# Low parts of the input weights kept in DRAM in the first half and loaded from there in the second

## Chip, cores and metric

The kernel runs on one core of a Trainium2 chip. The metric is the time of one execution on the device in microseconds (us). Three runs of the kernel before took 2506.31, 2506.98 and 2509.43 us.

## What is computed

One step of a streaming encoder layer with 1024 prompt tokens and 32 tokens of a running stream, model width 2048. Cut to what matters here:

```
xn   = rms_norm(x, norm_g)
proj = xn @ w_in                     # 2048 x 8320: q, k, v, gates, RWKV r/k/v, LoRA
q, k = rope(rms_norm(q)), rope(rms_norm(k))
att  = diff_attention(q, [past_k, k], [past_v, v])      # chunked causal mask
rw   = RWKV-7 recurrence over r, k, v, decay, a         # solved in chunks of 64 tokens
out  = x + [att * silu(g_att) ; rw * silu(g_rw)] @ w_out
```

All is float32 at the interface.

## The kernel before

**Tiling.** The tokens are cut into two halves: A has 544 tokens (512 of the prompt and the 32 of the running stream), B has 512. Columns of `w_in` come in 65 tiles of 128 (`f` = 0 to 64), those of `w_out` in 16. A projection of one tile (`proj`) multiplies the 16 x 128 rows of `w_in` into a PSUM bank `pj`. Half A is projected in two chunks of 288 and 256 tokens (`CHUNKS`), half B in one of 512. Both operands are split into a rounded high part of type fp32r and the rest, also fp32r; each of the 16 steps is three matmuls: high weight by high x (`wh`, `xh`), high weight by low x (`wh`, `xl`), low weight by high x (`wl`, `xh`).

**Weights.** The 16 steps come in four groups. For each group `load_w` (L238) loads 128 x 512 raw weights into `wr` (two slots) on the POOL queue, and `split_w` makes `wh` on ACT (L234) and `wl` on VectorE (L235), three slots each. So a group is 12 matmuls per chunk, and a slot of `wh` or `wl` comes free when TensorE is through with the group three before. Every tile of `w_in` is loaded and split twice, once in each half: 2 x 65 x 4 = 520 groups. Those of `w_out` for half A go the same way (64 groups); for half B `load_w2` loads pairs.

```
def split_w(raw):
    wh = T([128, 4, 128], "wh", F32R, bufs=3)
    wl = T([128, 4, 128], "wl", F32R, bufs=3)
    S.copy(wh, raw)
    V.tensor_tensor(wl, raw, wh.bitcast(F32), op=ALU.subtract)
```

**Order of the work.** Sixteen units (`u`), eight of each half, follow one another; unit `u` projects q, k, v, the attention gate, r, k, v and the RWKV gate of head pair `i`. Between the groups of a projection `pump` emits pieces of attention and of the recurrence of this and the unit before, by hand-set latencies (`LAT`) on a clock `clk` that counts TensorE's work. A scheduler then orders each engine's queue; `load_w` has high priority in it. An engine's queue is in order: an instruction that waits holds all behind it. SP issues nearly all transfers other than raw weights (`dma`, L184, and `dmq`, L112).

**The recurrence.** In `rw_down` each unit has two parts (`sub`). Products of TensorE are masked into `MM` (L784); 32 x 32 blocks of it go out to DRAM (`dm`), come back four times as `ms`, and VectorE inverts them in 31 steps of two instructions, `tm` (L803) and `ts` (L805), from a start `ts<-tinit`. The result goes out as `dt` (four stores) and comes back as `TT`, `t0q` and `t1q` for `rw_chain`, whose matmuls write the bank `ch`. `ms`, `ts` and `TT` have one slot each.

**Keys.** `qk_task` rotates q and k with a copy of rows (`t<-t`), and sends the low part of k into `Ks` by two copies (`Ks<-t`, L112); the score matmuls `sc<-Ks,Qd` read that.

**Between the halves.** At the end of unit 7 the normed x of half B is loaded (`t<-xB`) and split in place of A's, then the LoRA tile (`f` = 56) of half B is projected. Spans below are microseconds from the start of the execution: half A's projections run to about 1060, half B's to about 2085, then `w_out` follows for A and for B.

Of the kernel before, what the change touches and what calls it, by code (L numbers as in the profile page):

```python
# [12 lines left out]
F32R = mybir.dt.float32r  # L13
# [6 lines left out]
D = 2048  # L20
# [26 lines left out]
def build(tc, I, O):  # L47
    nc = tc.nc
# [7 lines left out]
    def T(shape, tag, dt=F32, bufs=1):  # L56
        cnt[0] += 1
        return sb.tile(shape, dt, tag=tag, name=f"{tag}_{cnt[0]}", bufs=bufs)
# [122 lines left out]
    def dma(out, in_):  # L181
        if out.dtype == F32R:
            out, in_ = out.bitcast(F32), in_.bitcast(F32)
        nc.sync.dma_start(out, in_)  # L184
# [35 lines left out]
    for z in (Qlo, wulo, TTb):  # L220
        G.memset(z.bitcast(F32), 0.0)

    mixd = [dr.tile([16, 128, n], F32, name=f"mixd{i}") for i, n in enumerate((NA, NB))]
    kpast = dr.tile([NH, 128, 2, 512], F32R, name="kpast")
    Spast = dr.tile([NP, 128, 64], F32, name="Spast")
# [5 lines left out]
# [4 lines that stand above are left out]
        V.tensor_tensor(wl, raw, wh.bitcast(F32), op=ALU.subtract)  # L235
        return wh, wl

    def load_w(wsrc, g, q=nc.gpsimd):  # L238
        with tc.high_priority():
            raw = T([128, 4, 128], "wr", bufs=2)  # L240
            q.dma_start(raw, wsrc[:, g * 512:(g + 1) * 512].rearrange("p (k f) -> p k f", k=4))  # L241
            return split_w(raw)

    def load_w2(wsrc, g):
        with tc.high_priority():
# [16 lines left out]

    RAW = ["Ks", "Vt", "E0", "E1", "rsg", "AR", "BK", "ms", "UV", "rk", "ca", "MM", "AR", "P3", "v", "rsg"]
    BUFS = dict(AR=2, MM=2, rsg=2, t=4)
    wpre = {0: load_w(I["w_in"][56], 0, nc.sync)}
    raw = []
    acc = T([128, NA], "asg")
    for k, tag in enumerate(RAW):
        xr = T([128, NA], tag, bufs=BUFS.get(tag, 1))
        dma(xr, I["xA"][:, k, :])  # L270
        raw.append(xr)
        if k % 4 == 0 and k < 8:
            wpre[k // 4 + 1] = load_w(I["w_in"][56], k // 4 + 1, nc.sync)
        split_x(k, xr, col(P_NG, k))
    for k, xr in enumerate(raw):
        s2 = T([128, NA], "p3", bufs=P3B) if k else acc
# [78 lines left out]
            p, r = (t.rearrange("p (a b) -> p a b", b=blocks) for t in (p, r))  # L355
        V.tensor_tensor(out, p, r, op=ALU.mult)

    def proj(wsrc, chunks, ws=None, nxt=None, pairs=False, banks=None):
        banks = banks or [PT("pj", 3) for _ in chunks]
        if len(chunks) == 2:  # L360
            order = [(0, 0), (0, 1), (1, 0), (1, 1), (0, 2), (0, 3), (1, 2), (1, 3)]
        else:
            order = [(0, g) for g in range(4)]
        ws = ws or {}
        for o, (b, g) in enumerate(order):
            if g not in ws:
                if pairs:
                    ws.update(load_w2(wsrc, g))
                else:
                    ws[g] = load_w(wsrc, g)  # L370
            wh, wl = ws[g]
            c0, n = chunks[b]
            for k in range(4 * g, 4 * g + 4):
                for m, (w, x) in enumerate(((wh, XH), (wh, XL), (wl, XH))):
                    mm(banks[b][:, :n], w[:, k % 4, :], x[k][:, c0:c0 + n],
                       start=(k == 0 and m == 0), stop=(k == KT - 1 and m == 2))
                if k < KT - 1:
                    if k % 4 == 3 or (k % 2 == 1 and n == 512):
                        pump()
                    else:  # L380
                        chs.run()
            if nxt and all(g != h for _, h in order[o + 1:]):
                for k in range(4 * g, 4 * g + 4):
                    nxt(k)
        return [(banks[b], c0, n) for b, (c0, n) in enumerate(chunks)]
# [17 lines left out]
    low, high = slice(0, 64), slice(64, 128)  # L403
# [263 lines left out]
    def lora(half, ws=None):  # L667
        ncnk = (9, 8)[half]
        spare = scores2()
        banks = proj(I["w_in"][56], CHUNKS[half], ws, banks=None if half else [spare[:, 0, :], spare[:, 1, :]])  # L670
        Lt = T([128, ncnk, 64], "p3", bufs=P3B)
        shift_tile(half, ncnk, banks, 24, Lt)
        S.activation(Lt[0:64], Lt[0:64], AF.Tanh)
        tc.keep_in_program_order(S.preload_act_table_set("natural_log_exp_and_others"))
        W = ncnk * 64
        Lf = Lt.rearrange("p c t -> p (c t)")
        Ls = T([128, 2, W], "lora", F32R)
        ll = T([128, W], "p3", F32R, bufs=P3B)
        for w in range(2):
            rows = (low, high)[w]  # L680
            S.copy(Ls[rows, w, :], Lf[rows])
            V.tensor_tensor(ll[rows], Lf[rows], Ls[rows, w, :].bitcast(F32), op=ALU.subtract)
        dma(Ls[64:128, 0, :], ll[0:64])
        dma(Ls[0:64, 1, :], ll[64:128])
        return Ls
# [311 lines left out]
    def out_proj(half, f, nxt=None):  # L997
        n = (NA, NB)[half]
        xr = T([128, n], "t", bufs=4)
        dma(xr, I["xA" if half == 0 else "xB"][:, f, :])  # L1000
        for (p, c0, m) in proj(I["w_out"][f], CHUNKS[half], nxt=nxt, pairs=half == 1):
            V.tensor_tensor(xr[:, c0:c0 + m], p[:, :m], xr[:, c0:c0 + m], op=ALU.add)
        dma(O["yA" if half == 0 else "yB"][f], xr)

# [15 lines left out]
    for u in range(16):  # L1020
        half, i = divmod(u, 8)
        n, ncnk, chunks = (NA, NB)[half], (9, 8)[half], CHUNKS[half]
        if u == 8:
            rb_b()
            ready["am"] = clk[0]
            load_rope(1)
            drain(los, ("decay", 7))
            Lt = lora(1)
        sa = dict(offs=[0, 128, 288, 416] if half == 0 else [0, 128, 256, 384])
        sr = dict()  # L1030
        srs.append(sr)
        los.add(("decay", u), rw_decay(half, i, sr, Lt))
        for sub in range(2):
            dns.add(("down", u, sub), rw_down(half, i, sub, sr))
            chs.add(("chain", u, sub), chain_when_down(half, i, sub, sr))
            pos.add(("post", u, sub), rw_post(half, i, sub, sr))

        def q_stage():
            banks = proj(I["w_in"][i], chunks)
            qks.add(("q", u), qk_task(0, half, i, qk_start(0, banks, n), sa))  # L1040

        def k_stage(prev):
            banks = proj(I["w_in"][8 + i], chunks)
            drain(qks, (prev, u))
            qks.add(("k", u), qk_task(1, half, i, qk_start(1, banks, n), sa))

        def v_stage(prev):
            banks = proj(I["w_in"][16 + i], chunks)
            drain(qks, (prev, u))
            qks.add(("v", u), v_task(half, i, banks, sa))  # L1050

        def ga_stage():
            banks = proj(I["w_in"][24 + i], chunks)
            if u:
                drain(ats, ("att", u - 1))
            sg = T([128, n], "asg")
            silu(sg, banks)
            sa["sg"] = sg

        def rw_stage(t):  # L1060
            banks = proj(I["w_in"][32 + 8 * t + i], chunks)
            if t == 0:
                if u:
                    drain(dns, ("down", u - 1, 1))
                sr["rk_"] = T([128, 2, ncnk, 64], "rk")
            rk = sr["rk_"]
            if t < 2:
                shift_tile(half, ncnk, banks, 8 * t + i, rk[:, t])
                if t == 1:
                    if half == 0:  # L1070
                        G.memset(rk[:, 1, 8, 32:64], 0.0)
                    sr["rk"] = rk
                return
            if u:
                drain(chs, ("vread", u - 1))
            v = T([128, ncnk, 64], "v")
            shift_tile(half, ncnk, banks, 16 + i, v)
            sr["v"] = v

        def gr_stage():  # L1080
            banks = proj(I["w_in"][57 + i], chunks,
                         nxt={7: source(I["xB"], True), 15: source(mixd[0], False)}.get(u))
            if u > 1:
                drain(pos, ("post", u - 2, 1))
            sg = T([128, n], "rsg", bufs=2)
            silu(sg, banks)
            sr["sg"] = sg

        att_stages = [(q_stage,), (v_stage, "q"), (k_stage, "v")] if half == 0 else [
            (q_stage,), (k_stage, "q"), (v_stage, "k")]  # L1090
        for stage, *args in att_stages:
            stage(*args)
            pump()
        ats.add(("att", u), att_task(half, i, sa))
        if u == 5:
            ats.add("stats", stats_task())
        ga_stage()
        drain(qks, ("k" if half == 0 else "v", u))
        pump()
        for t in range(3):  # L1100
            rw_stage(t)
            pump()
        gr_stage()
        pump()
# [109 lines left out]
```

## Time and profile before

| | us |
|---|---|
| runs, median of three (lowest to highest) | 2506.98 (2506.31 to 2509.43) |
| profiled execution | 2504.47 |
| its span | 2502.7 |
| TensorE (PE) busy | 2443.2 |
| VectorE (DVE) busy | 1864.0 |
| ACT busy | 1370.3 |
| moved by DMA | 286.72 MB |

Busy time is the time in which at least one instruction of the engine was under way. Matmuls are pipelined and their ends are modelled, so that TensorE can pause for a tenth of a microsecond or two without a gap in its busy time. A wait is put down to what came last before the waiting instruction started.

### The profile page before, as it was taken

How to read it: one execution, taken by the hardware profiler on the slowest of the kernel's cores; microseconds unless marked ns; L12 is line 12 of the kernel's file. 1: busy time of each engine (PE TensorE's matmuls, PEld its weight loads, DVE VectorE, ACT ScalarE, POOL GpSimd, SP SyncE). 2: the span in 40 equal slices, each digit the busy share in tenths (PEclk: the TensorE clock that was granted, in tenths of full speed). 3: DMA queues.
4: the chain of work that ended last, by engine and by line, in shares of the span. 5: the costliest groups of instructions: out<-in, count | busy, mean ns of one | idle time of the engine just before them, and what ended most of it. 6: DMA issues, size and time to landing. Idle time of an engine off the chain costs nothing.

```text
span 2502.7 us, 49026 instructions
## 1 busy us (share of the span) xinstructions
PE 2443.2 (98%) x17124; PEld 2163.9 (86%) x17124; DVE 1864.0 (74%) x5716; ACT 1370.3 (55%) x3286; POOL 453.8 (18%) x1070
## 2 busy tenths in 40 slices
PE   8999999999999999999999999999999999999999
PEld 7999999999999999977777787878787878999887
DVE  7577778788877878778888787878787878643432
ACT  7446465655556665656655565656565656332321
POOL 1212121211212121211111112121211111111100
PEclk9999999999999999999999999999999999999999
DMA  5343333434243525353333333333333344544443
GB/s 181 107 119 90 93 104 96 118 86 120 85 121 123 151 74 149 103 147 94 111 90 95 106 98 103 97 107 90 108 95 109 92 126 146 171 152 136 139 149 104
DMA packets 198919, 286.72 MB, mean 115 GB/s; under 512 B 102352, under 2 KB 116176, under 8 KB 198672
## 3 DMA queue, kind: packets, MB, share of 16 engines
q0 software_dynamic: 51088, 169.12, 22.5%
q1 hardware_dynamic: 147584, 114.47, 16.2%
q8 instruction: 135, 2.21, 0.4%
q14 instruction: 112, 0.92, 0.1%
HBM read 228.11 MB, written 37.51 MB: 106 GB/s over the span
## 4 chain that ended last, share of the span: by engine, by line
PE 69%; DVE 15%; DMA 7%; issue 4%; ACT 4%; POOL 0%; SPq 0%; DVEq 0%; ACTq 0%; POOLq 0%
PE pj L102 54%; PE ch L102 5%; PE am L102 4%; DVE wl L235 3%; PE sc L102 2%; DVE tm L803 2%; DVE ts L805 2%; PE Y L102 2%; DMA wr<-w_in 2%; ACT wh L234 1%; DMA Ks<-t 1%; PE sc L107 1%; PE am L107 1%; DMA p<-wup 1%; DMA wr<-w_out 1%
## 5 line engine op out<-in xcount | busy, mean ns | idle before, releaser
L102 PE MATMUL pj<-xh,wh 128*128 128x288 f32 (+2 forms) x3856 | 1292.4, 335 | 1.9 <-ACT wh L234 1.7
L102 PE MATMUL pj<-xh,wl 128*128 128x288 f32 (+2 forms) x3856 | 1253.4, 325 | 0.1
L102 PE MATMUL pj<-xl,wh 128*128 128x256 f32 (+2 forms) x3856 | 1250.5, 325 | 1.2 <-DVE xl L256 1.2
L102 PEld LDWEIGHTS pj<-xh,wl 128*128 128x128 f32 x3856 | 726.2, 188 | 55.2 <-issue 1.2
L102 PEld LDWEIGHTS pj<-xh,wh 128*128 128x128 f32 x3856 | 727.9, 189 | 53.0 <-ACT wh L234 2.6
L102 PEld LDWEIGHTS pj<-xl,wh 128*128 128x128 f32 x3856 | 728.1, 189 | 45.1 <-DVE xl L256 1.6
L234 ACT CAST wh<-wr 128x512 fp32r<-128x512 f32 x584 | 360.9, 618 | 497.6 <-PE pj L102 431.0
L235 DVE TENSOR_TENSOR wl<-wr,wh 128x512 fp32r<-128x512 f32 x584 | 400.6, 686 | 193.0 <-ACT wh L234 164.4
L241 POOL DMA_DIRECT2D wr<-w_in x517 | 277.9, 538 | 1400.3 <-DVE wl L235 568.7
L803 DVE TENSOR_TENSOR tm<-ts,ms 64x54 f32<-64x54 f32 (+35 forms) x992 | 198.9, 201 | 16.4 <-DMA ts<-tinit 2.3
L805 DVE TENSOR_TENSOR ts<-tm,ts 64x54 f32<-64x54 f32 (+35 forms) x992 | 199.1, 201 | 15.8 <-DVE tm L803 0.3
L933 ACT ACTIVATE SP<-Sw,PL 64x64 f32<-64x64 f32 x256 | 88.3, 345 | 44.2 <-DVE Sw L942 39.0
L235 DVE TENSOR_TENSOR wl<-MM,wh 128x512 fp32r<-128x512 f32 x64 | 44.0, 689 | 88.7 <-ACT wh L234 88.7
L234 ACT CAST wh<-MM 128x512 fp32r<-128x512 f32 x64 | 39.6, 621 | 128.4 <-PE pj L102 124.3
L102 PEld LDWEIGHTS ch<-UV,MM 128*128 128x128 f32 (+1 forms) x1088 | 92.7, 162 | 15.6 <-DVE UV L937 11.1
L102 PE MATMUL ch<-UV,MM 128*128 128x64 f32 (+1 forms) x1088 | 102.6, 246 | 3.5 <-DVE UV L937 3.3
L942 DVE SCALAR_TENSOR_TENSOR Sw<-ch,PL,SP 64x64 f32<-64x64 f32 x256 | 70.5, 275 | 32.1 <-PE ch L102 27.4
L611 ACT ACTIVATE E<-sc,sm 128x640 f32<-128x640 f32 (+3 forms) x64 | 61.0, 954 | 40.3 <-DVE sm L610 40.1
L102 PE MATMUL sc<-Ks,Qd 128*128 128x512 f32 (+2 forms) x224 | 74.1, 342 | 6.5 <-DMA Ks<-t 6.3
L102 PE MATMUL am<-Vt,E 128*128 128x128 f32 (+1 forms) x592 | 79.9, 277 | 0.0
L102 PEld LDWEIGHTS am<-Vt,E 128*128 128x128 f32 (+1 forms) x592 | 71.7, 189 | 5.4 <-ACT E L626 2.0
L930 DVE TENSOR_TENSOR xs<-ch,MM 64x64 f32<-64x64 f32 x272 | 58.2, 214 | 23.6 <-ACT RS L927 19.9
(314 smaller groups left out, 3227.3 us busy)
## 6 DMA issues: line engine op xcount, KB each, us to landing
wr<-w_in POOLq DMA_DIRECT2D x517, 256.0 KB, 3.3
wr<-w_out POOLq DMA_DIRECT2D x64, 256.0 KB, 3.6
MM<-w_out POOLq DMA_DIRECT2D x32, 512.0 KB, 4.2
t<-xB SPq DMA_DIRECT2D x32, 256.0 KB
ms<-dm SPq DMA_DIRECT2D x96, 64.0 KB
t<-t SPq DMA_DIRECT2D x64, 68.0 KB
t<-mixd SPq DMA_DIRECT2D x16, 272.0 KB
t<-xA SPq DMA_DIRECT2D x16, 272.0 KB
```

The source lines that it names most:

```text
L102: PE.matmul(out, lhsT, rhs, start=start, stop=stop)
L107: PE.transpose(out, in_, idn)
L234: S.copy(wh, raw)
L235: V.tensor_tensor(wl, raw, wh.bitcast(F32), op=ALU.subtract)
L241: q.dma_start(raw, wsrc[:, g * 512:(g + 1) * 512].rearrange("p (k f) -> p k f", k=4))
L611: S.activation(E[c][:, :nk], sc[:, :nk], AF.Exp, bias=mx[:, c:c + 1], scale=SCALE, accum_out=l[:, c:c + 1])
L803: V.tensor_tensor(tm, ts_[:, 0:qn, s:s + 1].to_broadcast([R * nb, qn, m]), ms[:, s:s + 1, s + 1:32].to_broadcast([R * nb, qn, m]), op=ALU. ...
L805: V.tensor_tensor(ts_[:, 0:qn, s + 1:32], tm, ts_[:, 0:qn, s + 1:32], op=ALU.add)
L930: V.tensor_tensor(xs[64 * h:64 * h + 64], ch[low, 64 * h:64 * h + 64], MM[low, c, h, 0:64], op=ALU.add)
L933: S.activation(SP[:, h, :], S_[hr, h, :], AF.Copy, scale=PL[hr, 0, gc:gc + 1])
L942: V.scalar_tensor_tensor(S_[hr, h, :], ch[low, 192 + 64 * h:256 + 64 * h], PL[low, h, gc:gc + 1], SP[:, h, :], ALU.mult, ALU.add)
```

## The change

In the first half, each `wl` that VectorE has made for a tile of `w_in` is also stored to a DRAM tile `wlow[f]`, by SP. In the second half `wl` isn't computed: SP loads it from `wlow[f]`; the raw weights are still loaded and ACT still makes `wh` from them. For `w_out` nothing changes. `proj` takes the number of the tile instead of its address.

```diff
+    wlow = [dr.tile([128, D], F32R, name=f"wlow{f}") for f in range(65)]
...
-    def load_w(wsrc, g, q=nc.gpsimd):
+    def load_w(wsrc, g, q=nc.gpsimd, keep=None, kept=None):
         with tc.high_priority():
             raw = T([128, 4, 128], "wr", bufs=2)
             q.dma_start(raw, wsrc[:, g * 512:(g + 1) * 512].rearrange("p (k f) -> p k f", k=4))
-            return split_w(raw)
+            if kept is not None:
+                wh = T([128, 4, 128], "wh", F32R, bufs=3)
+                wl = T([128, 4, 128], "wl", F32R, bufs=3)
+                dma(wl.rearrange("p k f -> p (k f)"), kept[:, g * 512:(g + 1) * 512])
+                S.copy(wh, raw)
+                return wh, wl
+            wh, wl = split_w(raw)
+            if keep is not None:
+                dma(keep[:, g * 512:(g + 1) * 512], wl.rearrange("p k f -> p (k f)"))
+            return wh, wl
...
-    def proj(wsrc, chunks, ws=None, nxt=None, pairs=False, banks=None):
+    def proj(f, chunks, ws=None, nxt=None, pairs=False, banks=None, w="w_in"):
+        wsrc = I[w][f]
+        low = wlow[f] if w == "w_in" else None
+        first = len(chunks) == 2
...
-                    ws[g] = load_w(wsrc, g)
+                    ws[g] = load_w(wsrc, g, keep=low if first else None, kept=None if first else low)
```

The callers of `proj` change only in what they hand over. VectorE's queue has 324 instructions `wl<-wr,wh` in place of 584; SP's has 260 `wlow<-wl` and 260 `wl<-wlow` more.

Three places in SP's queue follow, of before and of the change; `_` and digits number the tiles, the numbers of the two kernels don't correspond.

SP in unit 10, while it projects v and the attention gate, and VectorE ends one inverse and begins the next; before:

```order
L184 DMA dm_1_1_18972<-MM_18838 32x8x32 x2
L184 DMA mixd_84<-asg_17945 128x512
L112 DMA Qd_19094<-Qd_19094 64x512 x2
L112 DMA t_19183<-t_19174 32x512
L184 DMA dt_1_0_18573<-ts_18478 128x1x32 x4
L184 DMA ms_18975<-dm_1_1_18972 16x1024 x2
L184 DMA TT_79<-dt_1_0_18573 32x4x32 x4
L184 DMA t0q_18885<-dt_1_0_18573 128x2x32
L184 DMA t1q_18886<-dt_1_0_18573 128x2x32
L184 DMA ms_18975<-dm_1_1_18972 16x1024 x2
L184 DMA ts_18980<-tinit 64x256
```

and with the change, from the same `dm` on:

```order
L184 DMA dm_1_1_19297<-MM_19163 32x8x32 x2
L184 DMA wl_19517<-wlow_101 128x512
L184 DMA mixd_149<-asg_18270 128x512
L184 DMA ms_19300<-dm_1_1_19297 16x1024
L184 DMA wl_19535<-wlow_101 128x512
L184 DMA dt_1_0_18898<-ts_18803 128x1x32 x3
L184 DMA wl_19574<-wlow_101 128x512
L184 DMA dt_1_0_18898<-ts_18803 128x1x32
L184 DMA ms_19300<-dm_1_1_19297 16x1024
L184 DMA wl_19612<-wlow_101 128x512
L184 DMA TT_79<-dt_1_0_18898 32x4x32 x3
```

The loads `wl<-wlow` stand between the others one by one; one is behind the first `ms<-dm`, which was behind all four `dt<-ts`, and the stores of `dt` follow that load.

SP in the same unit, while it projects the RWKV tiles, at the end of the second inverse; before:

```order
L112 DMA Ks_19227<-t_19228 64x512 x2
L184 DMA vB<-t_19302 128x512
L184 DMA dt_1_1_19075<-ts_18980 128x1x32 x4
L184 DMA TT_79<-dt_1_1_19075 32x4x32 x4
L184 DMA t0q_19759<-dt_1_1_19075 128x2x32
L184 DMA t1q_19760<-dt_1_1_19075 128x2x32
L184 DMA ts_19974<-tinit 64x256
```

and with the change:

```order
L112 DMA Ks_19552<-t_19553 64x512
L184 DMA wl_19869<-wlow_117 128x512
L184 DMA wl_19915<-wlow_125 128x512
L184 DMA wl_19961<-wlow_125 128x512
L184 DMA dt_1_1_19400<-ts_19305 128x1x32 x2
L184 DMA wl_19991<-wlow_125 128x512
L184 DMA dt_1_1_19400<-ts_19305 128x1x32 x2
L184 DMA wl_20038<-wlow_125 128x512
L184 DMA t0q_20084<-dt_1_1_19400 128x2x32
L184 DMA t1q_20085<-dt_1_1_19400 128x2x32
L184 DMA ts_20299<-tinit 64x256
L184 DMA wl_20070<-wlow_133 128x512
```

A load now stands in the middle of the four `dt<-ts`, one behind them, and one behind `ts<-tinit`, the start of the inverse after that.

SP at the turn of the halves, around the LoRA tile of half B (`lora`) and the masked products of unit 7 (`dm`); before:

```order
L184 DMA mixd_83<-rsg_13621 128x544
L184 DMA dm_7_1_15851<-MM_15683 32x10x32 x2
L184 DMA dt_7_0_15317<-ts_15222 128x1x32 x4
L184 DMA lora_15826<-p_2520_15827 64x512 x2
L184 DMA ms_15854<-dm_7_1_15851 20x1024
```

and with the change:

```order
L184 DMA mixd_148<-rsg_13914 128x544
L184 DMA dm_7_1_16176<-MM_16008 32x10x32
L184 DMA wl_16405<-wlow_91 128x512
L184 DMA dm_7_1_16176<-MM_16008 32x10x32
L184 DMA dt_7_0_15638<-ts_15543 128x1x32
L184 DMA wl_16441<-wlow_91 128x512
L184 DMA dt_7_0_15638<-ts_15543 128x1x32 x2
L184 DMA wl_16479<-wlow_91 128x512
L184 DMA dt_7_0_15638<-ts_15543 128x1x32
L184 DMA lora_16151<-p_2520_16152 64x512 x2
```

Here a load stands between the two `dm<-MM`, and two between the `dt<-ts`.

## Rows read from the trace of the kernel before

**Rows 1.** The page: the span, busy time by engine, shares of the chain that ended last

```profile
span 2502.7 us, 49026 instructions
...
PE 2443.2 (98%) x17124; PEld 2163.9 (86%) x17124; DVE 1864.0 (74%) x5716; ACT 1370.3 (55%) x3286; POOL 453.8 (18%) x1070
...
PE pj L102 54%; PE ch L102 5%; PE am L102 4%; DVE wl L235 3%; PE sc L102 2%; DVE tm L803 2%; DVE ts L805 2%; PE Y L102 2%; DMA wr<-w_in 2%; ACT wh L234 1%; DMA Ks<-t 1%; PE sc L107 1%; PE am L107 1%; DMA p<-wup 1%; DMA wr<-w_out 1%
```

**Rows 2.** Stretches: length, busy PE, PEld, DVE, ACT, POOL; clock, DMA share, GB/s

```profile
100.00:1060.00 960.00, 939.13 (x8051) 904.51 (x8050) 767.09 (x2476) 564.38 (x1471) 190.18 (x497) 1.00 0.37 107
1060.00:2085.00 1025.00, 1008.79 (x5816) 808.63 (x5814) 840.25 (x2650) 613.19 (x1442) 188.61 (x410) 1.00 0.37 104
1060.00:1070.00 10.00, 9.79 (x68) 8.85 (x67) 9.73 (x31) 6.90 (x15) 1.61 (x3) 1.00 0.82 262
```

**Rows 3.** Waits of PE and PEld, 1060 to 2085 us: sum, times, longest

```profile
PE sc L102 <- DMA Ks<-t: 4.6, 7, 1.3
PE ch L102 <- DVE xs L930: 3.5, 8, 1.7
PE pj L102 <- ACT wh L234: 1.7, 1, 1.7
...
PEld sc L102 <- DMA Ks<-t: 5.9, 6, 1.1
```

**Rows 4.** Lines 235 and 241 from 1060 to 2085 us: durations, waits, landing

```profile
L235 DVE TENSOR_TENSOR wl<-wr,wh x259: 662/687/694, 1060.8 to 2083.4; 128x512 fp32r<-128x512 f32 x130
...
  ACT wh L234: 52.7, 50
...
DMA to landing us min/median/max: 3.0/3.2/5.1
```

**Rows 5.** Timeline of SP, DVE and PE in unit 4: start, us, instruction

```profile
604.35 3.36 SPq L184 DMA_DIRECT2D dt<-ts  x4
...
609.48 0.68 DVE L235 TENSOR_TENSOR wl<-wr,wh 128x512 fp32r<-128x512 f32 x1
...
626.06 0.38 PE L102 MATMUL ch<-u0q,mq 32*32 32x32 f32 x20
```

**Rows 6.** Timeline of PE: last matmul of one group, third of the group three later

```profile
1370.09 0.39 PE L102 MATMUL pj<-xh,wl 128*128 128x512 f32 x1
...
1376.55 0.39 PE L102 MATMUL pj<-xh,wl 128*128 128x512 f32 x1
```

**Rows 7.** Timeline of DVE: last product of the first inverse

```profile
1376.79 0.16 DVE L803 TENSOR_TENSOR tm<-ts,ms 64x8 f32<-64x8 f32 x1
```

**Rows 8.** Timeline of PE, the same two matmuls for place B

```profile
1414.21 0.39 PE L102 MATMUL pj<-xh,wl 128*128 128x512 f32 x1
...
1424.27 0.40 PE L102 MATMUL pj<-xh,wl 128*128 128x512 f32 x1
```

**Rows 9.** Timeline of SP: the stores of the second inverse

```profile
1425.86 2.53 SPq L184 DMA_DIRECT2D dt<-ts  x4
```

**Rows 10.** Stretches of the two inverses, line 235 alone: length, busy DVE

```profile
1333.00:1377.00 44.00, 7.01 (x11) 1.00 0.36 108
1390.00:1426.00 36.00, 6.43 (x10) 1.00 0.30 92
```

**Rows 11.** Timeline of SP at the turn of the halves

```profile
1101.71 0.84 SPq L184 DMA_DIRECT2D dm<-MM  x2
```

**Rows 12.** Timeline of PE there: third matmul of the group

```profile
1101.15 0.39 PE L102 MATMUL pj<-xh,wl 128*128 128x512 f32 x1
```

**Rows 13.** The chain that ended last, 1392 to 1405 us: start, us, what

```profile
1393.44 0.69 DVE wl L235
...
1396.59 0.60 DVE wl L235
...
1399.51 0.60 DVE wl L235
...
1400.88 3.74 DMA Ks<-t
```

More of the change, by code (lines that the diff above doesn't have):

```diff
@@ L264, in build @@
     BUFS = dict(AR=2, MM=2, rsg=2, t=4)
-    wpre = {0: load_w(I["w_in"][56], 0, nc.sync)}
+    wpre = {0: load_w(I["w_in"][56], 0, nc.sync, wlow[56])}
     raw = []
@@ L272, in build @@
         if k % 4 == 0 and k < 8:
-            wpre[k // 4 + 1] = load_w(I["w_in"][56], k // 4 + 1, nc.sync)
+            wpre[k // 4 + 1] = load_w(I["w_in"][56], k // 4 + 1, nc.sync, wlow[56])
         split_x(k, xr, col(P_NG, k))
@@ L669, in lora @@
         spare = scores2()
-        banks = proj(I["w_in"][56], CHUNKS[half], ws, banks=None if half else [spare[:, 0, :], spare[:, 1, :]])
+        banks = proj(56, CHUNKS[half], ws, banks=None if half else [spare[:, 0, :], spare[:, 1, :]])
         Lt = T([128, ncnk, 64], "p3", bufs=P3B)
@@ L1000, in out_proj @@
         dma(xr, I["xA" if half == 0 else "xB"][:, f, :])
-        for (p, c0, m) in proj(I["w_out"][f], CHUNKS[half], nxt=nxt, pairs=half == 1):
+        for (p, c0, m) in proj(f, CHUNKS[half], nxt=nxt, pairs=half == 1, w="w_out"):
             V.tensor_tensor(xr[:, c0:c0 + m], p[:, :m], xr[:, c0:c0 + m], op=ALU.add)
@@ L1038, in q_stage @@
         def q_stage():
-            banks = proj(I["w_in"][i], chunks)
+            banks = proj(i, chunks)
             qks.add(("q", u), qk_task(0, half, i, qk_start(0, banks, n), sa))
         def k_stage(prev):
-            banks = proj(I["w_in"][8 + i], chunks)
+            banks = proj(8 + i, chunks)
             drain(qks, (prev, u))
@@ L1047, in v_stage @@
         def v_stage(prev):
-            banks = proj(I["w_in"][16 + i], chunks)
+            banks = proj(16 + i, chunks)
             drain(qks, (prev, u))
@@ L1052, in ga_stage @@
         def ga_stage():
-            banks = proj(I["w_in"][24 + i], chunks)
+            banks = proj(24 + i, chunks)
             if u:
@@ L1060, in rw_stage @@
         def rw_stage(t):
-            banks = proj(I["w_in"][32 + 8 * t + i], chunks)
+            banks = proj(32 + 8 * t + i, chunks)
             if t == 0:
@@ L1080, in gr_stage @@
         def gr_stage():
-            banks = proj(I["w_in"][57 + i], chunks,
+            banks = proj(57 + i, chunks,
                          nxt={7: source(I["xB"], True), 15: source(mixd[0], False)}.get(u))
```

## The prediction

> **What bounds the kernel now.** I read the busy shares first. TensorE is busy for 98% of the span and the projections' matmuls alone make 54% of the chain that ended last [rows 1]; VectorE, whose work the change cuts, is busy for 74%. So VectorE is not the bound, and an edit pays only where TensorE stands still. Next I read the table of stretches. From 1060 to 2085 us, where the second half's input projections run, TensorE is busy for 1008.79 of 1025.00 us [rows 2]: 16.2 us of idle time is all that a faster VectorE can win there, apart from pauses shorter than the modelled ends of the matmuls. From 100 to 1060 us it is idle for 960.00 - 939.13 = 20.9 us.
>
> Then the wait lists of that second stretch show what TensorE stands still for: the key copy that ends in Ks (4.6 us in 7 waits, and 5.9 us on its weight loads), the chain's xs from VectorE (3.5 us), and smaller ones [rows 3].
>
> **What is removed.** VectorE loses 260 subtractions of 687 ns in the second half, 178.6 us, and with them its waits for the cast wh (52.7 us in 50 waits) [rows 4]. That is 231 of 1025 us of VectorE time, and almost none of it is on TensorE's path. What can come back is TensorE's waits for VectorE results. Bounds: nothing, and the whole 16.2 us. I take **-7 us**, a bit under half, since the list in [rows 3] is about half VectorE and half transfers and casts. The POOL queue's load of the next raw weights no longer waits for the subtraction either; ACT, which needs them, mostly waits for TensorE to free a slot, so I cost that at nothing.
>
> **What is added in the first half.** SP issues 260 stores of 256 KB, each of which waits for its subtraction, and everything behind it on SP waits too. An example: the inverse's result dt leaves at 604.35 us; in the new order the store of a piece that VectorE writes at 609.48 stands ahead of it, so dt leaves about 609.48 + 0.68 + 0.4 = 610.6, 6.2 us later. The matmul that reads what comes of it starts at 626.06 [rows 5], some 21 us after dt left, so this is covered; if that cover were gone, seven such units would cost 7 x 6.2 = 43 us. I expect no wait for the slots of wl either: there are three, and a store starts when its piece is written, while TensorE has still to read the piece in both chunks. Bounds: 0, and half of the stretch's idle time again, 10 us. I take **+2 us**.
>
> **What is added in the second half.** Each piece of wl is now loaded by SP. The load waits until TensorE is through with the piece three groups before, and everything behind it on SP waits with it; and it waits behind all that stands ahead. A group of 12 matmuls takes 2.8 us alone and about 4 with other work between, so a load has two groups, 5.6 to 8 us, to be issued and to land. For landing I take the raw load's median of 3.2 us, with 3.0 and 5.1 as its ends [rows 4]. So SP may be held for only some 2 to 4 us at a wrong place. The order has two such places in each unit.
>
> Place A: the load for one group stands behind the first ms<-dm. Its slot is free at 1370.09 + 0.39 = 1370.5 and TensorE reads it at 1376.55 [rows 6]. But ms is free for ms<-dm only after the last product of the previous inverse, 1376.79 + 0.16 = 1376.95 [rows 7]. With the issue of ms (0.5 us) the load would leave at 1377.5, land at 1380.7 and be 4.1 us late.
>
> Place B: a load stands between the second and third dt<-ts. Its slot is free at 1414.6, it is read at 1424.27 [rows 8], and dt leaves only at 1425.86, two of four taking 1.3 us [rows 9]: it would land at 1427.1 + 3.2 = 1430.3, 6.0 us late.
>
> Were nothing else changed, that is 10.1 us a unit, and 81 us for the eight inverses that run in this stretch. But both waits are for an inverse on VectorE, and the inverse is what VectorE is relieved for: 11 subtractions, 7.01 us, lie in the 44 us of the first and 10, 6.43 us, in the 36 us of the second [rows 10]. Then the first ends 7.0 us sooner, and its load lands 2.9 us in time; the second 6.4 us sooner, 0.4 us in time. With a landing of 5.1 us instead of 3.2 they would miss by 0 and by 1.5 us. So I take 1 us a unit, **+8 us**, between 0 and 81.
>
> The turn from one half to the other has such a place too: a load behind the first half of dm<-MM, which leaves at 1101.71 [rows 11]; 0.4 us for dm and 3.2 us for landing make 1105.3, and TensorE reads the piece at 1101.15 [rows 12], 4.2 us earlier. Here the product in MM waits on TensorE itself, so relief helps less; besides, the DMA engines are already busy for 0.82 of the time in the ten microseconds from 1060 [rows 2], where some four loads more come in. Bounds 0 and 15 us (two more such loads follow, behind dt and behind lora<-p); I take **+5 us**.
>
> Last, the key copy Ks<-t, 3.74 us on the chain in every unit [rows 13]. The three subtractions on the way to it in the chain, 0.69 + 0.60 + 0.60 = 1.9 us, go; but in the new order loads stand ahead of it on SP, and their 256 KB are on the way when it starts. At best its present wait goes (4.6 us over all units), at worst it is later by a whole landing less the 1.9 us, 1.3 us in each of eight units, 10 us. I take **+2 us**.
>
> A rule that speaks against the change bears on this. The trace shows small copies taking 3.74 us [rows 13] but no copy of SP behind a large load of SP's own. The Trainium skill, "DMA: Bandwidth & Descriptors", section "Queues, rings and completion order", says that descriptors of one ring are consumed in order, while rings of different queues take turns packet by packet. By it each of the eight key copies would wait for what is left of a whole load, which at that page's 27 GiB/s per engine is an estimated 0.6 us, 5 us in all instead of my 2; the sum would be +13. No row here shows it.
>
> **Sum.** -7 + 2 + 8 + 5 + 2 = +10 us. The profiled execution took 2504.5 us (span 2502.7 [rows 1]), so it would take 2514.5; the median of the runs, 2507.0, lies 2.5 us above it, so I say **2517 us**. 0.2%, about what a measurement of this kernel can tell from no change, is 5 us.
>
> **Rivals.** *Relief wins* (faster): the inverses end sooner by more than the subtractions' own time, because VectorE also no longer stops in its queue for the cast (52.7 us in all); no load is late, and TensorE's 16 us of waits shrink to a third. That gives -11 + 2 - 2 = -11 us, about 2496, and at most -16 + 2, 2493. For it speaks that places A and B come out in time even by my own sums; against it that they do so by 2.9 and 0.4 us, and that the longest wait of TensorE, for a copy on SP, gets more company. It decides if both inverses end 7 us or more sooner. Chance 0.24.
>
> *It cancels* (within 5 us): the loads are in time, and TensorE, as now, is fed by its own order: 2502 to 2512. For it speaks the 98%. Chance 0.22.
>
> *SP holds up everything* (slower by far): small copies wait behind loads that wait for TensorE, the inverses start later by what they were relieved of, and places A and B cost their 10.1 us in each unit: 81 + 5 + 2 + 2 = +90 us, 2597. For it: the order puts ms<-dm and ts<-tinit, from which an inverse starts, behind loads too. Against it: those loads wait only for slots that come free every 3 to 4 us. Chance 0.08. Half-way, with one of the two places missed in most units, it is some +45 us, 2552; that is in the range, with a chance of 0.12.
>
> My forecast, slower by 5 to 30 us, has what is left, 0.34. Together: faster 0.24, same 0.22, slower 0.54. The range reaches from 2493, all of the relief, to 2560, the half-way case with the first half's 10 us; what lies outside is most of the 0.08 and the edges.
>
> **What would show it.** Right: VectorE's busy time down by some 178 us in the second half and TensorE's not; in its wait list a new row, pj or its weight load waiting for the transfer wl<-wlow, of 5 to 30 us; the stretch that was 1025 us a little longer; the first half's stretch the same within a few us. The inverses (the products with ms) should end 5 to 8 us sooner in a unit. Wrong: no such row and a shorter second stretch (relief wins), or a first stretch longer by more than 10 us (then the stores hold SP where I saw cover), or rows of that kind of 50 us and more.

## The result, and the profile after

The changed kernel took 2544.93 us, the median of four runs (2539.79 to 2556.85); the kernel before took 2506.89 beside it (2506.31 to 2509.43). The ratio is 1.0158 (95% interval 1.0141 to 1.0175), 39.6 us slower by the ratio. Runs of the same pair later gave 1.0170 (1.0145 to 1.0194). The prediction had said slower, with 0.54, and 2517 us: the sign and the range (2493 to 2560) held, the size did not. The profiled execution is the slowest of the four, 2556.85 us, so that its stretches show some 12 us more of loss than the median.

The page of the changed kernel, for [rows 1]:

```profile
span 2555.1 us, 49713 instructions
...
PE 2458.2 (96%) x17124; PEld 2180.7 (85%) x17124; DVE 1724.4 (67%) x5456; ACT 1369.7 (54%) x3286; POOL 428.5 (17%) x1070
...
PE pj L102 49%; PE ch L102 5%; PE am L102 4%; DMA wr<-w_in 3%; PE sc L102 3%; DVE ts L818 2%; DVE tm L816 2%; DVE wl L236 2%; PE Y L102 2%; DMA Ks<-t 2%; DMA wr<-w_out 1%; PE sc L107 1%; ACT wh L235 1%; DVE MM L797 1%; PE am L107 1%
```

The stretches, for the first two of [rows 2] (columns as there). Half A's last stretch ends 46 us later, at 1106, half B's at 2138:

```profile
100.00:1106.00 1006.00, 969.87 (x8131) 927.67 (x8130) 770.75 (x2492) 567.49 (x1478) 186.61 (x507) 0.98 0.54 165
1106.00:2138.00 1032.00, 998.49 (x5813) 807.80 (x5812) 702.29 (x2390) 612.34 (x1441) 170.13 (x411) 1.00 0.57 169
```

So the loss is where the prediction had +2 us: the first stretch is 46 us longer (960 to 1006), the second 7 (1025 to 1032), though in the second VectorE is busy for 138 us less (840.25 to 702.29). TensorE's idle time in the second rises from 16.2 to 33.5 us, and its busy time falls by 10.3 us (1008.79 to 998.49). In the first, the DMA engines' mean share rose from 0.37 to 0.54 and the granted clock fell from 1.00 to 0.98; the added bytes are 256 KB in each of 260 stores.

What the raw weights did in the first stretch (line 242, the counterpart of line 241: who waited for it, and the landing; before the change the same view says 23.9 us in 8 waits, and 3.0/3.3/6.7):

```profile
  ACT wh L235: 71.6, 36
...
DMA to landing us min/median/max: 3.2/4.2/7.4
```

What TensorE waits for in the second stretch, for [rows 3]:

```profile
PE sc L102 <- DMA Ks<-t: 10.2, 7, 2.1
PE ch L102 <- ACT Ks L484: 6.0, 6, 1.5
PE Y L107 <- DVE MM L797: 3.8, 6, 2.8
...
PE pj L102 <- DMA wl<-wlow: 0.5, 1, 0.5
```

The loads that I feared most, wl arriving late at the projections, cost 0.5 us. TensorE's wait for the key copy Ks<-t rose from 4.6 to 10.2 us.

Three theories for the first half. **Bytes**: the stores share the way to DRAM with raw weights and with small copies, which land later, and what waits for them is late (no run separates the DMA engines from the DRAM behind them). **Queue**: a store that waits for VectorE holds SP, and with it the small transfers behind it. **Order**: the scheduler, given 260 more instructions, orders the other engines worse.

### The profile page after: what moved, and what is told of

Its sections match the earlier page's. It is cut to its first block, busy times and chain, and to the rows that moved or that the text cites. A ratio compares the mean times of both kernels' runs of the same rounds, so it can differ in the third digit from the quotient of the medians.

```text
span 2555.1 us, 49713 instructions
## 1 busy us (share of the span) xinstructions
PE 2458.2 (96%) x17124; PEld 2180.7 (85%) x17124; DVE 1724.4 (67%) x5456; ACT 1369.7 (54%) x3286; POOL 428.5 (17%) x1070
## 4 chain that ended last, share of the span: by engine, by line
PE 64%; DVE 15%; DMA 10%; issue 5%; ACT 4%; SPq 1%; POOL 0%; DVEq 0%; ACTq 0%; POOLq 0%
PE pj L102 49%; PE ch L102 5%; PE am L102 4%; DMA wr<-w_in 3%; PE sc L102 3%; DVE ts L818 2%; DVE tm L816 2%; DVE wl L236 2%; PE Y L102 2%; DMA Ks<-t 2%; DMA wr<-w_out 1%; PE sc L107 1%; ACT wh L235 1%; DVE MM L797 1%; PE am L107 1%
## 5 line engine op out<-in xcount | busy, mean ns | idle before, releaser
L102 PE MATMUL pj<-xh,wl 128*128 128x256 f32 (+2 forms) x3856 | 1261.4, 327 | 2.5 <-DVE wl L236 2.0
L236 DVE TENSOR_TENSOR wl<-wr,wh 128x512 fp32r<-128x512 f32 x324 | 222.8, 688 | 156.0 <-ACT wh L235 138.1
```

Of the source, the lines that this page charges most:

```text
L102: PE.matmul(out, lhsT, rhs, start=start, stop=stop)
```

## The experiments

### One half of the change at a time

Stores alone: `kept` is never given, so that the second half computes wl as before.

```diff
-ws[g] = load_w(wsrc, g, keep=low if first else None, kept=None if first else low)
+ws[g] = load_w(wsrc, g, keep=low if first else None, kept=None)
```

> Only the first half of the change: the 260 stores stay, the second half computes wl as before and loads nothing. In the profiled pair the first half is 46 us longer and the second 6.5 us longer. Traffic theory (the stores' bytes make the raw weights land later) and queue theory (small transfers on SP wait behind stores that wait for VectorE) both give the whole first-half loss here and nothing behind it: 2535 to 2553 us, first xh of half B at 1090 to 1101 us. If the first half's loss came from the loads or was a whim of one execution: 2505 to 2515.

Measured: 2547.44 us, ratio 1.0155 (1.0139 to 1.0171): the whole loss. Loads alone: four pieces of tile 56 are stored, and every load reads those.

```diff
+ws[g] = load_w(wsrc, g, keep=low if first and f == 56 else None,
+               kept=None if first or low is None else wlow[56])
```

> Only the second half of the change: the four pieces of one tile are stored, and every load of the second half reads those four (so the low parts of the other tiles are not theirs); 256 stores of the first half are left out. First half as before within 3 us; second half by the prediction's terms -7 + 8 + 5 + 2 = +8: 2513 to 2518. If the loads' traffic costs like that of the stores: 2535 and more. If relief of VectorE wins once the first half no longer runs late: 2496 to 2502.

Measured: 2527.11 us, 1.0078 (1.0048 to 1.0107), some 20 us. The casts Ks<-t of unit 0 and of unit 8 begin 3.8 and 9.4 us later than before; the rest, 11 us, is the second half's, which VectorE runs in the order of the changed kernel (2058 of 2064 instructions from the first cast Ks<-t of unit 8 to that of unit 15). The two parts do not add up (39 + 20 against 40), so I measured the whole beside the stores alone once more.

> The changed kernel once more, beside the kernel with stores alone in the same call: 2540 to 2550. By what the loads cost alone it should stand 8 to 15 us above the kernel with stores alone; the medians so far (2545 and 2547, of four runs each, from two calls) say no difference.

> The kernel with stores alone once more, as the base for the one before: 2543 to 2550.

Measured: 2546.57 (1.0170, 1.0145 to 1.0194) and 2540.85 (1.0155, 1.0134 to 1.0176). The loads and all that they relieve come to 1 to 6 us on top of the stores, which the intervals don't separate from nothing.

### Bytes, queue or order

Same 260 stores, but of one partition, 2 KB:

```diff
-dma(keep[:, g * 512:(g + 1) * 512], wl.rearrange("p k f -> p (k f)"))
+dma(keep[0:1, g * 512:(g + 1) * 512], wl[0:1].rearrange("p k f -> p (k f)"))
```

> As the kernel with stores alone, but each store writes one of the 128 partitions (2 KB instead of 256 KB); the same 260 instructions stand at the same places of SP's queue and wait for the same pieces. Queue theory: the time of the kernel with whole stores, 2535 to 2553, with ACT waiting for raw weights little more than before. Traffic theory: near the kernel before, 2505 to 2513, with the raw load's landing back at 3.3 us median and ACT's waits for it at some 25 us in the first half.

Measured: 1.0009 (0.9998 to 1.0020), 2 us. In the two traces ACT and VectorE run the same instructions in the same order throughout, TensorE too but for 18 of its 17124 places, and SP issues the same transfers in the same sequence. So queue and order are in both and together cost the 2 us, and the 37 us between the two kernels are the size of the stores alone: 256 KB in 128 packets instead of 2 KB in one. SP's waits for wl are even the longer in the quick one. SP of the kernel with small stores, 100 to 1062 us, then of that with whole stores, 100 to 1096 (sum, times, longest):

```profile
SPq L184 <- DVE wl L236: 254.8, 95, 8.1
```

```profile
SPq L184 <- DVE wl L236: 155.7, 65, 7.9
```

What the bytes do: line 242 in the same stretches, small stores first.

```profile
  ACT wh L235: 6.9, 4
...
DMA to landing us min/median/max: 3.0/3.3/6.3
```

```profile
  ACT wh L235: 54.5, 31
...
DMA to landing us min/median/max: 3.2/4.2/6.5
```

A raw load lands 0.9 us later, and ACT stops in its queue for it 31 times instead of 4. And the recurrence's small copies, at the same place of unit 1 (timeline, SP and VectorE), small stores first:

```profile
180.05 0.51 SPq L184 DMA_DIRECT2D t0q<-dt  x1
...
183.93 0.25 DVE L886 STREAM_TRANSPOSE u0q<-t0q 128x64 f32<-128x64 f32 x1 [1.69 <-DMA t0q<-dt]
```

```profile
190.68 0.37 SPq L184 DMA_DIRECT2D wlow<-wl  x1
...
191.62 0.45 SPq L184 DMA_DIRECT2D wlow<-wl  x1
...
192.60 0.51 SPq L184 DMA_DIRECT2D t0q<-dt  x1
...
197.97 0.25 DVE L886 STREAM_TRANSPOSE u0q<-t0q 128x64 f32<-128x64 f32 x1 [5.09 <-DMA t0q<-dt]
```

From issue to use it takes 3.9 us there and 5.4 here, behind two whole stores; VectorE, whose queue is in order, stands for 5.09 us. Over the first half its waits of this kind rise from 3.3 us in 3 to 15.2 us in 7 (100 to 1062 and to 1096 us).

TensorE then pauses longer, and after that its clock drops. Stretches of the kernel with whole stores (columns as in [rows 2]):

```profile
90.00:96.50 6.50, 2.34 (x17) 1.82 (x15) 4.05 (x9) 4.46 (x9) 0.71 (x2) 1.00 0.74 213
97.30:100.70 3.40, 3.40 (x18) 3.40 (x17) 1.71 (x5) 1.00 (x4) 0.54 (x1) 0.50 0.90 270
...
300.00:308.90 8.90, 5.96 (x54) 5.46 (x53) 7.00 (x25) 2.38 (x6) 1.08 (x2) 1.00 0.63 194
308.90:319.10 10.20, 10.06 (x38) 8.61 (x39) 5.17 (x22) 2.23 (x4) 0.54 (x1) 0.50 0.32 101
```

TensorE is busy for 2.34 of 6.50 us, then granted 0.50, which is 1.2 of 2.4 GHz. The first half has five such stretches, 23.8 us together, and a sixth of 3.4 us follows at 1114 us; with small stores there is one of 6.8 us. From the first cast Ks<-t of unit 0 to that of unit 8 the two kernels read:

```profile
82.60:1148.80 1066.20, 1043.41 (x8596) 984.16 (x8595) 843.27 (x2717) 624.00 (x1586) 202.90 (x542) 1.00 0.39 111
```

```profile
90.00:1184.20 1094.20, 1052.38 (x8579) 990.59 (x8578) 844.80 (x2716) 624.48 (x1586) 201.62 (x541) 0.99 0.55 164
```

Of these 28.0 us, 19.0 are idle time of TensorE (22.8 to 41.8) and 9.0 are the same matmuls taking longer, about half of the 20 us more at the lower clock. Another 7.4 us were lost before unit 0 (82.6 to 90.0).

The dose, in the same order of ACT's and VectorE's queues: 64 of 128 partitions.

```diff
+dma(keep[0:64, g * 512:(g + 1) * 512], wl[0:64].rearrange("p k f -> p (k f)"))
```

> As the kernel with stores alone, but each store writes 64 of the 128 partitions: 128 KB in 64 packets of 2 KB. The order of ACT's and VectorE's queues is word for word that of the stores of 256 KB (2544 us) and of 2 KB (2512 us). If the loss goes with the bytes: half way, 2524 to 2532. If a store costs by being there, or only from a threshold on: near one of the two ends.

Measured: 2530.41 us, 1.0110 (1.0096 to 1.0124). In us per 2507: 2 at 2 KB, 28 at 128 KB, 39 at 256 KB. It rises with the size, the first half of the bytes costing more than the second. Whole stores for every second tile only:

```diff
+ws[g] = load_w(wsrc, g, keep=low if first and f % 2 else None, kept=None)
```

> As the kernel with stores alone (2547 us, 39 more than before), but only tiles with an odd number are stored, 128 stores instead of 260, and not the LoRA tile at the start. Traffic theory, with each store delaying the raw load beside it by about its own time on the DMA engines: the loss goes with the bytes, some 17 to 22 us, 2525 to 2530. If it decides only above a certain load on the DMA engines: under 8 us. If one late load in two is enough to hold up the whole order: 30 us and more.

Measured: 2523.04, 1.0066 (1.0040 to 1.0091), 17 us. There are 131 stores, not 128: three pieces of the LoRA tile at the start are stored by a line that the edit leaves alone. The bytes are those of the stores of 128 KB, which cost 28 us; but VectorE's order differs from theirs from 56 us on, so that the 11 us between them have no one cause. Stores of 128 packets of 128 bytes:

```diff
+dma(keep[:, g * 512:g * 512 + 32], wl[:, 0, 0:32])
```

> As the kernel with stores alone, but each store writes the first 32 of a partition's 512 numbers: 128 packets as there, of 128 bytes instead of 2 KB, 16 KB a store. The order of the instructions is that of the stores of 256 KB and of 2 KB. If the bytes cost: 128-byte packets take some 13 ns on a DMA engine where 2 KB take 92, so a seventh of the 35 us that lie between those two kernels: 2514 to 2520. If the number of packets costs: 2540 and more.

Measured: 2521.31, 1.0072 (1.0055 to 1.0089), 18 us. The expectation was wrong in its premise: this kernel's VectorE queue was ordered anew (1787 of 2824 instructions of the first half stand in the sequence of the others). Raw loads landed nearly as before (median 3.4 us); whether the 18 us belong to the packets or to that order stays open.

Whole stores on another queue:

```diff
-dma(keep[:, g * 512:(g + 1) * 512], wl.rearrange("p k f -> p (k f)"))
+nc.gpsimd.dma_start(keep[:, g * 512:(g + 1) * 512].bitcast(F32),
+                    wl.rearrange("p k f -> p (k f)").bitcast(F32))
```

> As the kernel with stores alone, but the stores are issued on the POOL queue, which already waits for the same subtraction before it may load into the slot of the raw weights; SP's queue is that of before. Traffic theory: the same bytes, the same loss, 2535 to 2553. Queue theory: SP is free again, 2505 to 2515, plus what 260 more issues cost on POOL (the raw loads leave later by one issue each).

Measured: 2544.38, 1.0138 (1.0118 to 1.0158). Here SP's queue has no store in it, VectorE's order is nearly that of the kernel before (5652 of 5716 instructions), and the loss stays. The raw load lands at 3.3/3.9/7.9, ACT waits for it 78.0 us in 32. The Trainium skill, "DMA: Bandwidth & Descriptors", section "Issuing engines are not separate DMA queues", says that transfers of all issuing engines run on the same 16 DMA engines and interleave there. By that rule another queue frees no bandwidth; the run agrees, with 35 us against 39.

### Which late transfers count

Three slots for raw weights instead of two, with the stores and without. For room the table of sines is left out, so that both compute something else.

```diff
-raw = T([128, 4, 128], "wr", bufs=2)
+raw = T([128, 4, 128], "wr", bufs=3)
...
-ropes[half] = (cs, sn)
+ropes[half] = (cs, cs)
```

> The kernel before with three slots for raw weights instead of two; to make room the table of sines isn't kept (the table of cosines stands in its place, so q and k are rotated wrongly, and two transfers of 272 KB are left out). It is the base of the next kernel. ACT's 24 us of waits for raw weights in the first half go, TensorE gains little: 2500 to 2510.

> The kernel with stores alone, also with three slots for raw weights and without the table of sines. If the stores cost by the way of late raw weights (they land 0.9 us later, ACT stops in its queue for them and all behind it is late), a load that starts a group earlier covers this: within 10 us of the kernel with three slots and no stores. If they cost by small transfers of SP landing later in the traffic: still 30 us and more above it.

Measured: 2496.96 (0.9962, 0.9950 to 0.9975) and 2525.94 (1.0082, 1.0054 to 1.0110), 29 us apart. With the stores, ACT's waits for raw weights are down from 54.5 to 3.1 us (100 to 1085 us), and three quarters of the loss remain. VectorE's longest waits for transfers there:

```profile
DVE u0q L886 <- DMA t0q<-dt: 13.4, 7, 3.7
DVE tm L816 <- DMA ts<-tinit: 3.9, 4, 1.8
DVE tm L816 <- DMA ms<-dm: 2.1, 1, 2.1
```

and of the kernel with three slots and no stores (100 to 1060 us):

```profile
DVE u0q L873 <- DMA t0q<-dt: 9.3, 5, 2.9
```

So late raw weights look like the smaller part, some 10 of 39 us. The two kernels of this pair are not in the same order (about three quarters of VectorE's first half stand in one sequence), so that this figure is less sure than the 37 us. Where the rest comes from stays open. The small copies are late in the trace, but the three waits shown are together less than 10 us longer here than without stores (4 of them t0q<-dt), and the kernel before has 13.0 us in 6 waits for t0q<-dt (100 to 1060 us) at 2507 us, so such a wait need not cost TensorE its length. Nothing that I ran delays small copies alone. Would the third slot make a kernel faster than both? With the sines, and the room taken from p3 (`P3B = 2`):

> The kernel before with three slots for raw weights, and the sines kept; room is made by two slots instead of three for the short-lived tiles p3. The kernel that left the sines out ran 10 us faster than before, by late raw weights that ACT no longer waits for. If that was the slot's doing and p3's third slot is not needed: 2493 to 2500. If p3 then holds up the recurrence: 2510 and more. If the 10 us came from the two transfers of sines that were left out: 2503 to 2508.

Measured: 2506.07, 1.0012 (1.0001 to 1.0023): no gain. It runs up to 10 us ahead of the kernel before as far as unit 10 and has given it back by the first sum of w_out. That p3's missing slot takes it is likely, not shown; nor is it that the 10 us of the other pair were the slot's and not the sines'.

### The second half: relief against traffic

Loads alone, but of 64 KB, which stand for all four blocks of a piece:

```diff
-dma(wl.rearrange("p k f -> p (k f)"), kept[:, g * 512:(g + 1) * 512])
+dma(wl[:, 0, :], kept[:, g * 512:g * 512 + 128])
...
-return wh, wl
+return wh, wl[:, 0:1, :]
```

> As the kernel with loads alone, but each load brings 128 of 512 numbers a partition (64 KB), which stand for all four blocks of the piece, so the low parts are not those of the tile; instructions, waits and VectorE's relief as there. If the second half loses by its bytes alone, some 11 us at 256 KB: 3 us there and 4 at the start, less the relief of VectorE if there is any: 2505 to 2515. If it loses by SP's order, by loads that hold SP: 2522 to 2530 as with whole loads.

Measured: 2496.55, 0.9971 (0.9959 to 0.9984), 7 us faster than before and 27 faster than with whole loads. But the scheduler ordered this kernel's second half anew (about three quarters of VectorE's 2064 instructions there stand in the sequence of the kernel with whole loads), so the 27 us are not the bytes alone. What it shows is that 260 loads which hold SP need not cost the relief. Whole loads on POOL's queue:

```diff
-dma(wl.rearrange("p k f -> p (k f)"), kept[:, g * 512:(g + 1) * 512])
+nc.gpsimd.dma_start(wl.rearrange("p k f -> p (k f)").bitcast(F32),
+                    kept[:, g * 512:(g + 1) * 512].bitcast(F32))
```

> As the kernel with loads alone (2527 us, 19 more than before, some 11 to 15 of them in the second half), but the loads of wl are issued on the POOL queue behind the raw load; SP's queue in the second half is that of before. If the second half loses because SP's order holds up the key path (t<-t and Ks<-t behind loads): that loss goes, 2505 to 2513, and the start's 5 us stay. If it is the traffic that makes small transfers and raw loads late: still 2520 to 2530, with TensorE's waits for Ks<-t as there.

Measured: 2535.56, 1.0118 (1.0090 to 1.0146), 30 us slower. The loss needs no load on SP, though this kernel's order is new as well. TensorE's wait for Ks<-t is gone there (8.5 us in the kernel with SP's loads), but ACT waits 32.0 us in 21 for raw weights, which land at 3.0/4.1/7.1: on whichever queue the loads are, something else is late.

The relief by itself: the subtraction left out, wh in place of wl.

```diff
+if e == 0:
+    return wh, wh
```

> The kernel before, with the 260 subtractions of the second half left out and nothing in their place: the high part stands for the low part there, so the products are not the reference's. This is VectorE's relief alone, without transfer and without POOL. Prediction's term: 7 us faster (0 to 16). By the second half of the kernel with quarter loads: 8 to 12 us faster. If the quarter loads' gain was something else: no change.

Measured: 2490.06, 0.9935 (0.9919 to 0.9952), 16 us faster. This second half is in a new order, too: somewhat over half of VectorE's other instructions stand in the sequence of the kernel before. So the 16 us are the relief together with that order. And the subtraction moved to POOL, for all and for every second piece of the second half:

```diff
-V.tensor_tensor(wl, raw, wh.bitcast(F32), op=ALU.subtract)
+(e or V).tensor_tensor(wl, raw, wh.bitcast(F32), op=ALU.subtract)
```

> The kernel before, with nothing stored or loaded; the 260 subtractions of the second half run on POOL instead of VectorE. If VectorE's relief alone is worth what the kernel with quarter loads shows in its second half (some 9 to 12 us), and POOL takes little over VectorE's 0.69 us for one: 2493 to 2500. If POOL takes so long for one (2 us and more) that the raw load behind it in POOL's own queue and the piece itself come late: 2510 and more.

> As the one before, but only every second subtraction of the second half runs on POOL. Relief theory: half of its gain, 2499 to 2503. If POOL is slow for one but not too slow for every second: better than the one before.

Measured: 2624.98 (1.0494, 1.0479 to 1.0509) and 2584.87 (1.0324, 1.0308 to 1.0341). No way to the gain: one takes 1.29 us there against 0.69, and some of VectorE's small products take far longer beside it. POOL's subtraction, then VectorE's tm from 1100 to 2100 us (busy, mean ns), of the kernel with all on POOL; then tm of the kernel before:

```profile
L235 POOL TENSOR_TENSOR wl<-wr,wh x260: 1256/1285/4139, 1058.2 to 2206.8; 128x512 fp32r<-128x512 f32 x130
```

```profile
L803 DVE TENSOR_TENSOR tm<-ts,ms 64x60 f32<-64x60 f32 (+29 forms) x428 | 130.1, 304 | 12.6 <-DMA ts<-tinit 5.5
```

```profile
L803 DVE TENSOR_TENSOR tm<-ts,ms 64x54 f32<-64x54 f32 (+26 forms) x470 | 93.7, 199 | 5.6
```

The mean of 304 ns mixes two kinds. The 355 tm that meet no subtraction take 0.20 us, as before; the 57 that start during one take 0.94 us on the mean and end 0.07 us (median) after it. Timeline of the kernel with all on POOL:

```profile
1102.93 1.28 POOL L235 TENSOR_TENSOR wl<-wr,wh 128x512 fp32r<-128x512 f32 x1 [3.42 <-ACT wh L234]
...
1103.00 1.25 DVE L803 TENSOR_TENSOR tm<-ts,ms 64x24 f32<-64x24 f32 x1
...
1104.50 0.17 DVE L803 TENSOR_TENSOR tm<-ts,ms 64x16 f32<-64x16 f32 x1
```

The 27 copies UV<-ch out of PSUM that start during a subtraction take 0.23 us, as in the kernel before.

## Why the prediction was wrong

**The failed step is the first half's term, +2 us, bounds 0 to 10.** It measured 39 (35 to 43 by its interval). That step asked two things of the stores: what they hold up on SP, and whether they hold a slot of wl. Both it got right in the main: with the same stores at 2 KB the loss is 2 us, and the changed kernel's VectorE waits for a slot (wl <- wlow<-wl) for 4.4 us in 4 waits from 20 us on. What it left out is the 68 MB themselves. For the loads of the second half I did ask what they share with other transfers, for the stores never. The view that would have said so is [rows 2]: 68 MB in 1050 us are 65 GB/s beside the 107 that were there, at a share of 0.37 already. The upper bound, half of the stretch's idle time again, was taken from TensorE's idle time as it was, which bounds what can be won, not what can be lost. That 2545 us lies in the range is luck: the range went up to 2560 for late loads in the second half, with 10 us for the first.

**Relief, -7 (0 to -16).** It came out larger, 16 us (12 to 20 by its interval) when nothing takes its place, and not by the way that the term counted. The term was to come out of TensorE's 16.2 us of idle time, from its waits for VectorE. In the kernel without the subtraction the same stretch reads:

```profile
1060.00:2076.50 1016.50, 996.73 (x5815) 811.67 (x5815) 704.46 (x2391) 611.95 (x1441) 182.67 (x411) 1.00 0.37 105
```

It is 8.5 us shorter, but TensorE's idle time is 19.8 us in it, more than before; its busy time is 12 us less for as many matmuls (5815 against 5816). The changed kernel shows the same (10.3 us less busy, idle time up). The prediction set pauses too short for the busy time aside; whether the gain is those or the new order stays open. The inverse's 31 steps took 34.7 us on the mean in the second half before and 26.5 after (first tm to last), 8 us sooner, where 5 to 8 were forecast; so this sign came true, and TensorE's idle time did not follow it. VectorE's busy time fell by 138 us, not 178: an instruction starts before the one ahead of it is through (in the trace of the stores alone a wl starts at 198.15 us and lasts 0.69 us, the next instruction starts at 198.76), so 260 durations are more than the busy time they free.

**Loads behind the inverses, +8 (0 to 81).** The mechanism did not happen: TensorE's projections waited 0.5 us for wl, once. The inverses ended sooner, as the relief in the prediction's own sum allowed.

**The turn, +5 (0 to 15).** Not seen, net of any relief there: from unit 7 to unit 8 (first casts Ks<-t) the changed kernel lost 1.1 us in the first profile and 0.7 in the second.

**The key copy, +2 (up to 10).** TensorE's wait for it rose by 5.6 us (4.6 to 10.2), and 6.0 us in which the chain's ch waits behind ACT's cast into Ks came in. The rule that the prediction cited from the Trainium skill ("DMA: Bandwidth & Descriptors", "Queues, rings and completion order": one ring is consumed in order) would have made it 5. By that rule the copy should come free when the loads are on another queue, and there the wait did go; but it is gone as well in the kernels with loads of 64 KB on SP and without the subtraction, all in orders of their own, so that no run shows the ring as its cause.

Together the second half's terms were +8 with the turn, and measured 1 to 6: -16 of relief, and so, if that holds in this order too, 17 to 22 of what the loads cost (27 in the kernel with loads alone: 11 in the second half, and the 16). That this is their traffic fits the rows (raw weights landing at a median of 3.6 us instead of 3.2, at 3.9 and 4.1 in the two kernels with loads alone, and ACT's waits for them up from 10.3 to 20.5 us; the key copy) and is not shown with all else equal, as it is for the stores. The rival "relief wins" was right that the inverses end sooner and that there is something to win, and missed that the loads take it back; that TensorE's waits shrink no run shows. "SP holds up everything" is refuted, on both sides. The tests that the prediction set itself were the right ones: a first stretch longer by more than 10 us was to mean that the stores hold SP. It was longer, and it was not SP.

## What to carry to other kernels

Price the bytes of an added transfer as you price its instruction: look at the DMA share of the stretch, and at every transfer there that somebody waits for, and ask what each microsecond of later landing does to a queue that is in order. To tell a busy queue from busy DMA engines, keep every instruction and cut the bytes. Then compare the orders of the engines: where they stay (stores of 2 KB and 128 KB), the difference is the traffic; where the scheduler orders anew (stores of 16 KB, loads of 64 KB), it is not that alone. A shorter busy time of one engine is no gain by itself, and a gain need not show in another's idle time. Recomputing 0.69 us on an engine with room to spare can be cheaper than fetching 256 KB, even when no engine waits for the fetched piece itself.

## What was not expected of the hardware

At a mean DMA share of 0.55 a load of 256 KB landed after 4.2 us (median) instead of the 3.3 at 0.38, and a kernel whose TensorE is busy for 96 to 98% of the span took 1.5% longer by stores on which almost nothing waits. Pauses of TensorE of a few us were followed by 3.4 to 10.2 us at a granted clock of 0.50, so that a pause cost more than itself: 9 us on top of 19. And POOL was no free engine: VectorE's small products that started while it subtracted took 0.94 us instead of 0.20 and ended with the subtraction, while VectorE's copies out of PSUM kept their 0.23 us. The Trainium skill, "SBUF — State Buffer", section "SBUF: two separate sides", says that the two engines share a pair of ports, which one at a time holds; the rows agree with such a lock, and no run here shows the ports themselves.
